# The memory layer of a decode step: the sample's products with the states as tiled matmuls (unsplit fp32 on four column tiles, fp32r on four row tiles)

## The chip, the core and the metric

The kernel runs on one core of one Trainium2 chip. The metric is device time in microseconds (us) of one execution, lower is better. A profile of one execution is shown beside it: its span runs from the first to the last instruction. PE is the matrix engine (PEld its weight loads, which overlap its products), DVE the vector engine, ACT the scalar engine, POOL the general-purpose engine, SP the engine that issues the DMAs here.

## What is computed

One inference step of a two-layer decoder trunk (layer 0: a gated MLP that mixes tokens in chunks; layer 1: an mLSTM matrix memory; a gated MLP with a causal convolution behind each) on a prompt of 256 tokens and on a sample of 8 sequences with 8 new tokens each. All weights are shared. The change lies in layer 1, the memory layer. Per head (8 heads, key width 128, value width 256) the reference does, cut to what matters:

```python
b = jnp.cumsum(fc, axis=-1)
D = where(mask, b[..., :, None] - b[..., None, :] + ic[..., None, :], -inf)
inter = b + m[..., None]
m_t = jnp.maximum(inter, jnp.max(D, axis=-1))
w_intra, w_inter = jnp.exp(D - m_t[..., None]), jnp.exp(inter - m_t)
sc = jnp.einsum('bhtd,bhsd->bhts', qc, kc) * w_intra
num = w_inter[..., None] * einsum('bhtd,bhde->bhte', qc, C) + einsum('bhts,bhse->bhte', sc, vc)
den = w_inter * jnp.einsum('bhtd,bhd->bht', qc, n) + jnp.sum(sc, axis=-1)
h = num / jnp.maximum(jnp.abs(den), jnp.exp(-m_t))[..., None]
g = jnp.exp(bL[..., None] - b + ic - m_new[..., None])
kg = kc * g[..., None]
C_new = decay[..., None, None] * C + jnp.einsum('bhsd,bhse->bhde', kg, vc)
n_new = decay[..., None] * n + jnp.sum(kg, axis=2)
```

The prompt starts from an empty memory. The sample's 8 sequences each bring an old state C (128 x 256 per head) that their 8 queries must meet, and each leaves a new one.

## The kernel before

All activations are kept transposed, 320 tokens wide (256 of the prompt, then 64 of the sample). A weight matrix is used in blocks of 128 output columns: `block` (L151) multiplies 8 slices of 128 x 128 with the activations. fp32 values are split into a high and a low half of type fp32r, and three products (high x high, high x low, low x high) make one fp32 product; that is `chunk` (L143), 24 matmuls of 320 columns for a block. The weights' split is `prefetch` (L104): SP loads a raw block, ACT casts the high half (L125), DVE subtracts for the low half (L126), into three buffers.

The order of the matmuls is the order in which the program issues them (`mm`, `tr` and the helpers pin them). Other instructions are placed by a planner from its own costs; `behind_split` (L130) puts a group behind the last weight split. PSUM has eight banks: three for blocks (`psm`), five for all else (`psa`).

Layer 1 (`layer_b`) first makes the gate rows (`gates`, L508) together with the six blocks of head 0, and then goes through the heads. For head h six blocks are made: two for q and k with a convolution (`qk_epi`), two for v, two for the output gate. Among these blocks stands the memory work of heads h and h - 1:

- `scores` (L628): the decay weights and q k products; it also puts the sample's queries, high half and low half apart, into `Qz`, where each sequence has 128 columns, zero except for its own 8 + 8 rows.
- `state_in`, `state_split` (L704, L711): four loads of two states each, each split by ACT (L715) and DVE (L717) into a high and a low half.
- `inter` (L720): for each sequence two products, `Qz` slice against the high and the low half of its state, 258 columns, into one PSUM bank `num`. 16 matmuls for a head.
- `numer` (L733): 11 products of the scores with the values. `stats` (L747) normalises; `finish` (L813) transposes the result (six transposes) for the out-projection.
- `k_nat`, `v_nat` (L679, L665): keys and values turned to rows. The sample's keys, high halves in partitions 0 to 63 and remainders in 64 to 127, are put into `kgz`: for each sequence a copy with all other rows zero (POOL, L695).
- `state_sample` (L791): for each sequence two products of 256 columns, `kgz` slice against the high and the low half of the values, into a bank `pcs`; DVE adds the decayed old state (L803) and SP stores it. 16 matmuls for a head, four at a time.
- `state_prompt` (L776): the prompt's new state, and the sample's new normaliser with one product of 8 columns (L783).

Head 0 has no work of an earlier head beside it: behind the blocks of `gates` come its three gate transposes `pt` (L585), then at once scores, key and value transposes. Behind the last head the order is: a part of the out-projection, `inter`, `numer`, a block, `stats`, a block, `finish`, `state_sample`.

Of the kernel before, what the change touches and what calls it, by code (L numbers as in the profile page):

```python
# [37 lines left out]
class Net:  # L38
# [10 lines left out]
    def tr(self, out, in_, ident):  # L49
        self.pin(self.nc.tensor.transpose(out, in_, ident))  # L50

# [132 lines left out]

    def tokens(self, a, t):

        return a[:, (0, P, T - P)[t]:(P, TP, T)[t]]

    def norm_cols(self, parts=None, twice=False):
# [4 lines left out]
        pv = pc[:, 0:6].rearrange("p (t e) -> p t e", e=2)  # L194
        for t in range(3):
            for i, a in enumerate(parts):
                self.mm(pv[:, t, :], self.tokens(a, t), self.ones[:, :2], i == 0, i == len(parts) - 1)
# [3 lines left out]
        if twice:  # L201
            nc.scalar.copy(ms[:64, 2:3], ms[64:, 2:3])
        nc.gpsimd.tensor_tensor(rc, ms, self.mhalf.to_broadcast([P, 3]), op=ALU.pow)
        self.rc = rc

    def norm_row(self):
# [4 lines left out]
        for t, (c0, cs) in enumerate(((0, slice(0, P)), (P, slice(0, P)), (TP, slice(64, P)))):  # L211
            nc.vector.tensor_scalar(dg[:, c0:c0 + cs.stop - cs.start], self.ident[:, cs], self.rc[:, t:t + 1], None, op0=MULT)
# [265 lines left out]
    def layer_b(self):  # L478
# [5 lines left out]
        with ExitStack() as ctx:  # L484
# [10 lines left out]
            mk = lp.tile([P, NB], F32, name="mk")  # L495
# [10 lines left out]


            def gates(rp):  # L508
# [4 lines left out]
                RS = rp.tile([P, 384], F32, name="RS")  # L513
# [5 lines left out]
                nc.sync.dma_start(mk, I["blk"])  # L519
                nc.gpsimd.memset(RS, 0.0)  # L520
# [50 lines left out]
                nc.vector.tensor_copy(mkr, mk)  # L571
# [6 lines left out]
                nc.vector.tensor_copy(RS[:, T:384], RS[:, TP:T])  # L578
# [3 lines left out]
                o_epi(0, 1, self.block(KD, self.x_rhs))  # L582
                pt = self.psa.tile([P, 512], F32, tag="pa", name="pt")
                for t in range(3):
                    self.tr(pt[:, t * P:(t + 1) * P], RS[:, t * P:(t + 1) * P], self.ident)  # L585
                nc.vector.tensor_copy(colsT, pt[:, :384].rearrange("p (t e) -> p t e", e=P)[:, :, :96])
                nc.vector.tensor_scalar(colsT[:, :, 32:40], colsT[:, :, 32:40], 0.5 * KSC, None, op0=MULT)

# [3 lines left out]
            def qk_epi(h, j, ps):  # L592
# [16 lines left out]
                qs = lp.tile([P, 384], F32, tag="qs", name="qs", bufs=2)  # L609
# [7 lines left out]
                if j:  # L617
                    nc.scalar.copy(qs[:, T:384], qs[:, TP:T])
# [3 lines left out]
            def v_epi(h, j, ps):  # L622
                vT = lp.tile([P, 384], F32, tag="vT", name="vTb", bufs=2)
                nc.scalar.copy(vT[:, :T], ps[:, :T])
                nc.scalar.copy(vT[:, T:384], ps[:, TP:T])
                S[h].setdefault("vT", []).append(vT)

            def scores(h):  # L628
# [8 lines left out]
                mm(sc[:, 384:448], k[:, TP:384], q[:, TP:T], True, True)  # L637
                w = hp.tile([P, 448], F32, tag="w", name="w", bufs=1)
                for (n, o, c0, c1, t) in ((P, 0, 0, TP, 0), (P, TP, P, TP, 1), (64, 384, TP, T, 2)):
                    nc.scalar.activation(w[:n, o:o + c1 - c0], pb[:n, c0:c1], AF.Exp, scale=-1.0, bias=colsT[:n, t, h:h + 1])  # L640
# [3 lines left out]
                w3 = seg(w[:64, 384:448])  # L644
                nc.gpsimd.affine_select(w3, w3, pattern=[[-NS, NB], [0, NS]], compare_op=ALU.is_ge, fill=0.0, base=0,
                                        channel_multiplier=1)
                nc.gpsimd.affine_select(w3, w3, pattern=[[NS, NB], [1, NS]], compare_op=ALU.is_ge, fill=0.0, base=0,
                                        channel_multiplier=-1)
                dec = hp.tile([P, NB], F32, tag="dec", name="dec", bufs=2)
                nc.vector.tensor_copy(dec, pb[:, 384:392])  # L650
# [8 lines left out]
                nc.vector.scalar_tensor_tensor(Pf[:, :384], sc[:, :384], 0.25 * KSC, w[:, :384], op0=MULT, op1=MULT)  # L659
                nc.vector.scalar_tensor_tensor(Pf[:64, 384:], sc[:64, 384:448], 0.25 * KSC, w[:64, 384:], op0=MULT, op1=MULT)  # L660
                self.split(Ph[:, :384], Pl, Pf[:, :384])
                self.split(Ps[:64, :64], Ps[:64, 64:], Pf[:64, 384:])
                s["P"] = (Ph, Pl, dec)

            def v_nat(h):  # L665
# [6 lines left out]
                for t in range(3):  # L672
                    dst = dsts[t]
                    sc = self.rc[:, t:t + 1]
                    n = P if t < 2 else 64
                    nc.scalar.activation(vh[:, t, :DV], dst[:, :DV], AF.Copy, scale=sc)
                    nc.vector.scalar_tensor_tensor(vl[:n, t, :DV], dst[:n, :DV], sc[:n], vh[:n, t, :DV].bitcast(F32), op0=MULT, op1=SUB)

            def k_nat(h):  # L679
# [3 lines left out]
                for t in range(3):  # L683
                    self.tr(pk[:, t * P:(t + 1) * P], ks[:, t * P:(t + 1) * P], self.ident)
                kgh = hp.tile([P, 2, P], F32R, tag="kgh", name="kgh", bufs=1)
                kgl = hp.tile([P, 2, P], F32R, tag="kgl", name="kgl", bufs=1)
                kgt = hp.tile([P, P], F32R, tag="kgt", name="kgt", bufs=1)
                kgs = hp.tile([P, P], F32R, tag="kgs", name="kgs", bufs=1)
# [143 lines left out]
            with tc.tile_pool(name="rows", bufs=1) as rp:  # L832
                gates(rp)
# [252 lines left out]
```

## Time and profile before

| what | value |
|---|---|
| device time, 3 runs | 980.11, 980.13, 981.29 us (median 980.13) |
| profiled execution, span | 979.3 us |
| lying around the span, against the median | 0.8 us |
| PE busy | 965.4 us (99%) |
| weight loads busy | 959.8 us (98%) |
| DVE, ACT, POOL busy | 701.6, 510.9, 101.8 us (72, 52, 10%) |
| granted PE clock, mean | 0.997 |
| layer 1 in the span | about 432 to 722 us |

The profile gives no other time of the profiled execution than its span. In a timeline a row is the start of an instruction, its length, engine, line, operation, output and inputs, shape, and a count where equal ones follow each other; in square brackets stands how long the engine stood idle before it and what ended that. A matmul's length is longer than its share of the engine, since matmuls are pipelined: what one costs is the distance from its start to the next start. A plain fp32 matmul shows as two instructions with two weight loads, one behind the other.

### The profile page before, as it was taken

What the parts mean: (1) busy time and instruction counts of PE and PEld (TensorE: products, weight loads), DVE (VectorE), ACT (ScalarE), POOL (GpSimd) and SP (SyncE); (2) the same over time, 40 slices, a digit from 0 to 9 for tenths busy, and PEclk for the clock granted to TensorE, in tenths of its full rate; (3) what the DMA queues carried; (4) which work ended last, traced back from release to release, by engine and by line L of the source; (5) the groups of instructions that cost most, each with busy time, mean ns of one, the idle gap of its engine ahead of it and who ended that gap; (6) DMA issues with size and microseconds to landing.
All of it is one profiled execution on the core that took longest, in us unless ns stands there. A gap on an engine that the chain in (4) does not pass through costs nothing.

```text
span 979.3 us, 17600 instructions
## 1 busy us (share of the span) xinstructions
PE 965.4 (99%) x6695; PEld 959.8 (98%) x6695; DVE 701.6 (72%) x1353; ACT 510.9 (52%) x919; POOL 101.8 (10%) x270
## 2 busy tenths in 40 slices
PE   8999999999999999999999999999999999999996
PEld 8999999999999999999999999999999999999996
DVE  6747985567777764458999888788787777775442
ACT  6437444445544543448766766565655455444332
POOL 0200000010000000014332121111101000000000
PEclk9999999999999999999999999999999999999998
DMA  8635444444444455555565655544364444445541
GB/s 276 195 127 158 136 136 152 151 137 152 147 147 153 147 155 149 158 172 169 178 192 177 207 182 167 180 158 152 113 213 155 150 152 151 151 146 148 142 133 54
DMA packets 55802, 154.71 MB, mean 158 GB/s; under 512 B 6614, under 2 KB 17494, under 8 KB 55718
## 3 DMA queue, kind: packets, MB, share of 16 engines
q1 hardware_dynamic: 55718, 153.59, 49.5%
q8 instruction: 53, 0.87, 0.4%
q14 instruction: 31, 0.25, 0.1%
HBM read 141.63 MB, written 11.94 MB: 157 GB/s over the span
## 4 chain that ended last, share of the span: by engine, by line
PE 85%; issue 9%; DVE 2%; DMA 1%; POOL 1%; ACT 1%; SPq 0%; DVEq 0%; POOLq 0%; ACTq 0%
PE pm L47 76%; PE num L47 2%; PE pcs L47 2%; PE pmix L47 1%; DVE wl L126 1%; DMA xT<-in_xT 1%; PE pvt L50 1%; PE phn L50 1%; PE psc L47 1%; PE pCp L47 1%; PE pv L50 0%; DMA C<-in_C 0%; POOL Cl L717 0%; PE pg L47 0%; PE pc L47 0%
## 5 line engine op out<-in xcount | busy, mean ns | idle before, releaser
L125 ACT CAST wh<-raw 128x1024 fp32r<-128x1024 f32 (+3 forms) x254 | 257.5, 1014 | 351.8 <-PE pm L47 198.2
L47 PE MATMUL pm<-xh,wh 128*128 128x320 f32 x1344 | 419.6, 312 | 2.0 <-ACT wh L125 1.8
L47 PE MATMUL pm<-xh,wl 128*128 128x320 f32 x1344 | 415.7, 309 | 0.2 <-DVE wl L126 0.2
L47 PE MATMUL pm<-xl,wh 128*128 128x320 f32 x1344 | 415.3, 309 | 0.0
L126 DVE TENSOR_TENSOR wl<-raw,wh 128x1024 fp32r<-128x1024 f32 (+3 forms) x254 | 303.1, 1194 | 115.9 <-ACT wh L125 113.3
L47 PEld LDWEIGHTS pm<-xh,wh 128*128 128x128 f32 x1344 | 252.6, 188 | 3.1 <-ACT wh L125 2.7
L47 PEld LDWEIGHTS pm<-xh,wl 128*128 128x128 f32 x1344 | 252.3, 188 | 0.7 <-DVE wl L126 0.6
L47 PEld LDWEIGHTS pm<-xl,wh 128*128 128x128 f32 x1344 | 252.6, 188 | 0.2
L47 PE MATMUL pm<-yh_f,wh 128*128 128x320 f32 x352 | 109.0, 310 | 0.0
L47 PE MATMUL pm<-yh_f,wl 128*128 128x320 f32 x352 | 108.5, 308 | 0.0
L47 PE MATMUL pm<-yl_f,wh 128*128 128x320 f32 x352 | 108.5, 308 | 0.0
L47 PEld LDWEIGHTS pm<-yl_f,wh 128*128 128x128 f32 x352 | 66.1, 188 | 0.0
L47 PEld LDWEIGHTS pm<-yh_f,wh 128*128 128x128 f32 x352 | 66.1, 188 | 0.0
L47 PEld LDWEIGHTS pm<-yh_f,wl 128*128 128x128 f32 x352 | 66.1, 188 | 0.0
L400 DVE SCALAR_TENSOR_TENSOR fcv<-fpad,vecs,fcv 128x336 f32<-128x336 f32 x88 | 49.6, 565 | 2.2 <-ACT fcv L398 0.7
L223 DVE TENSOR_TENSOR xT<-pm,xT 128x320 f32<-128x320 f32 x40 | 19.6, 490 | 42.6 <-PE pm L47 42.6
L47 PE MATMUL pm<-yhb,wl 128*128 128x320 f32 x128 | 39.6, 309 | 0.5 <-DVE wl L126 0.5
L47 PE MATMUL pm<-yhb,wh 128*128 128x320 f32 x128 | 39.7, 310 | 0.0
L47 PE MATMUL pm<-yh_a,wh 128*128 128x320 f32 x128 | 39.6, 309 | 0.0
L47 PE MATMUL pm<-ylb,wh 128*128 128x320 f32 x128 | 39.5, 309 | 0.0
L47 PE MATMUL pm<-yh_a,wl 128*128 128x320 f32 x128 | 39.5, 308 | 0.0
L47 PE MATMUL pm<-yl_a,wh 128*128 128x320 f32 x128 | 39.5, 308 | 0.0
(251 smaller groups left out, 1265.6 us busy)
## 6 DMA issues: line engine op xcount, KB each, us to landing
raw<-in_f_up SPq DMA_DIRECT2D x88, 512.0 KB, 3.3
raw<-in_b_win SPq DMA_DIRECT2D x48, 512.0 KB, 3.6
raw<-in_a_win SPq DMA_DIRECT2D x30, 512.0 KB, 3.8
raw<-in_f_dn SPq DMA_DIRECT2D x32, 448.0 KB, 3.4
C<-in_C SPq DMA_DIRECT2D x32, 258.0 KB, 4.1
raw<-in_a_wo SPq DMA_DIRECT2D x16, 512.0 KB, 3.9
raw<-in_f_dn SPq DMA_DIRECT2D x16, 512.0 KB, 3.5
out_Cs<-C SPq DMA_DIRECT2D x32, 256.0 KB, 2.9
```

Source lines behind the costliest of these rows:

```text
L47: self.pin(self.nc.tensor.matmul(out, lhsT, rhs, start=start, stop=stop))
L50: self.pin(self.nc.tensor.transpose(out, in_, ident))
L125: self.last_split = nc.scalar.copy(wh[:, :kn, :], raw[:, :kn, :])
L126: self.last_low = nc.vector.tensor_tensor(wl[:, :kn, :], raw[:, :kn, :], wh[:, :kn, :].bitcast(F32), op=SUB)
L223: self.nc.vector.tensor_tensor(x, ps[:, :T], x, op=ADD)
L400: nc.vector.scalar_tensor_tensor(cv, pd[:, i:i + NC], self.vec(w + i * KF), cv, op0=MULT, op1=ADD)
```

## The change

The sample's 64 tokens are laid out anew wherever they stand in partitions: four groups of 32 partitions, in each 16 tokens (two sequences) twice (`spread`, `twice`). In the lower copy the high halves are to stand, in the upper one the remainders. The mask array `blk` gets five more columns for that, and a new small array `mxb` masks the sample's score weights.

- `inter` takes the states as fp32, unsplit: for each of four groups g and each of its two sequences i one product of 32 query columns against 258 state columns, into partitions 32 g to 32 g + 31 of the bank. That is 8 plain fp32 matmuls for a head, on four column tiles. `state_split` goes away, and with it the halves of the states; `Qz` is fp32 and has 320 columns.
- `state_sample` takes keys and values from 32 partitions: for each sequence of a group and each half of the values one product for each of the four groups, 256 columns, into four PSUM banks at once. 16 fp32r matmuls for a head, on four row tiles. `kgz` goes away; `kz` is made by four DVE instructions.
- The old `state_sample` is cut in two: the matmuls, and `state_out` (DVE and the store).
- `state_prompt` makes the normaliser with two products instead of one.
- The order within a head changes: `inter` and `state_sample` of head h stand together at its end (`hand_over`), `numer` and `state_prompt` behind the first block of the next head (`close`, one block earlier than before), `k_nat` at once behind `scores`, `finish` ahead of an output-gate block instead of behind it. `state_in` stands behind the second block.
- The first block of head 1 is made inside `gates`, ahead of the transposes `pt`.

```diff
+    def tr_some(self, out, in_, ident):
+        self.pin(self.nc.tensor.matmul(out, in_, ident, start=True, stop=True, is_transpose=True))
...
+    @staticmethod
+    def spread(x):
+        return x.rearrange("p (g d s) -> p g d s", g=4, d=2)
+    @staticmethod
+    def twice(x):
+        return x.rearrange("p (g s) -> p g s", g=4).unsqueeze(2).to_broadcast([P, 4, 2, 16])
...
                 o_epi(0, 1, self.block(KD, self.x_rhs))
+                ps = self.block(KD, self.x_rhs)
                 pt = self.psa.tile([P, 512], F32, tag="pa", name="pt")
...
             def scores(h):
-                qw = hp.tile([P, 64], F32, tag="qw", name="qw", bufs=1)
-                nc.vector.scalar_tensor_tensor(qw, q[:, TP:T], 0.5, pb[:, T:384], op0=MULT, op1=MULT)
-                Qd = Qz.rearrange("p (b e) -> p b e", e=136)
-                nc.scalar.copy(Qd[:, :, 0:8], seg(qw))
-                nc.vector.tensor_tensor(Qd[:, :, 64:72], seg(qw), Qd[:, :, 0:8].bitcast(F32), op=SUB)
+                Qd = Qz.rearrange("p (g i r) -> p g i r", g=4, i=2)[:, :, :, :NS]
+                nc.vector.scalar_tensor_tensor(Qd, q[:, TP:T].rearrange("p (g i t) -> p g i t", g=4, i=2), 0.5,
+                                               pb[:, T:384].rearrange("p (g i t) -> p g i t", g=4, i=2), op0=MULT, op1=MULT)
...
             def k_nat(h):
-                nc.gpsimd.tensor_tensor(kgz, kgs.bitcast(F32).unsqueeze(1).to_broadcast([P, NB, P]),
-                                        mk.unsqueeze(2).to_broadcast([P, NB, P]), op=MULT)
+                for i in range(2):
+                    nc.vector.tensor_scalar(kr[:, i, :], src, gm[:, 2 + i, h:h + 1], None, op0=MULT)
+                    nc.vector.scalar_tensor_tensor(kz[:, i, :], src, gm[:, i, h:h + 1], kr[:, i, :].bitcast(F32), op0=MULT, op1=SUB)
...
-            def state_split(h, i):
-                C0 = S[h]["C"][i]
-                Ch = hp.tile([P, 2, CW], F32R, tag="Ch", name="Ch", bufs=3)
-                Cl = hp.tile([P, 2, CW], F32R, tag="Cl", name="Cl", bufs=3)
-                nc.scalar.copy(Ch, C0)
-                (nc.vector if h or i < 2 else nc.gpsimd).tensor_tensor(Cl, C0, Ch.bitcast(F32), op=SUB)
...
+            def inter(h):
+                s = S[h]
+                s["num2"] = self.psa.tile([P, 512], F32, tag="pa", name="num")
+                for i in range(2):
+                    for g in range(4):
+                        mm(s["num2"][32 * g:32 * g + 32, :CW], Qz[:, 80 * g + 32 * i:80 * g + 32 * i + 32], s["C"][g][:, i, :],
+                           i == 0, False)
+            def state_sample(h):
+                s = S[h]
+                kz = s["kg"][2]
+                s["pcs"] = [self.psa.tile([P, 512], F32, tag="pa", name="pcs") for _ in range(4)]
+                for i in range(2):
+                    for v in (vh, vl):
+                        for g in range(4):
+                            r = slice(32 * g, 32 * g + 32)
+                            mm(s["pcs"][g][:, i * DV:(i + 1) * DV], kz[r, i, :], v[r, 2, :DV], v is vh, v is vl)
+            def state_out(h, g):
+                s = S[h]
+                dec, C0, pcs = s["P"][2], s["C"][g], s["pcs"][g]
                 for u in range(2):
+                    b = 2 * g + u
+                    nc.vector.scalar_tensor_tensor(C0[:, u, :DV], C0[:, u, :DV], dec[:, b:b + 1], pcs[:, u * DV:(u + 1) * DV],
+                                                   op0=MULT, op1=ADD)
+                nc.sync.dma_start(O["Cs"][h, :, 2 * g:2 * g + 2, :], C0[:, :, :DV])
...
-                mm(pc[:, 264:272], kgs, mkr, True, True)
+                for i in range(2):
+                    mm(pc[:, 264:272], kz[:, i, :], mkr, i == 0, i == 1)
...
+            def hand_over(h):
+                inter(h)
+                state_sample(h)
+                for g in (0, 1):
+                    state_out(h, g)
+            def close(h):
+                for g in (2, 3):
+                    state_out(h, g)
+                numer(h)
+                state_prompt(h)
+            state_in(0)
+            scores(0)
+            k_nat(0)
+            v_nat(0)
+            for h in range(1, NH):
+                last = h == NH - 1
+                ps = second if h == 1 else blk()
+                if h > 1:
+                    close(h - 1)
+                qk_epi(h, 0, ps)
+                early(h, 0)
+                ps = blk()
+                if h == 1:
+                    hand_over(0)
+                qk_epi(h, 1, ps)
+                early(h, 1)
+                state_in(h)
+                ps = blk()
+                if h == 1:
+                    close(0)
+                else:
                     with self.behind_split():
                         stats(h - 1)
+                v_epi(h, 0, ps)
+                early(h, 2)
+                ps = blk()
+                if h == 1:
+                    with self.behind_split():
+                        stats(0)
+                v_epi(h, 1, ps)
                 scores(h)
+                k_nat(h)
+                if h > 1:
+                    finish(h - 1)
                 early(h, 3)
+                if last:
+                    begin(0)
+                else:
+                    o_epi(h, 0, blk())
+                if h == 1:
+                    finish(0)
                 early(h, 4)
+                v_nat(h)
+                if not last:
                     o_epi(h, 1, blk())
+                    hand_over(h)
                 early(h, 5)
...
             begin(1)
-            inter(h, 1)
-            for i in (2, 3):
-                inter(h, i)
+            inter(h)
             numer(h)
...
             finish(h)
-            for i in range(4):
-                state_sample(h, i)
+            state_sample(h)
+            for g in range(4):
+                state_out(h, g)
             begin(2)
```

More of the change, by code (lines that the diff above doesn't have):

```diff
@@ L701, in k_nat @@
                     nc.vector.scalar_tensor_tensor(kgl[:, t, :], src, g, kgh[:, t, :].bitcast(F32), op0=MULT, op1=SUB)
-                s["kg"] = (kgh, kgl, kgs, kgz)
+                s["kg"] = (kgh, kgl, kz)
             def state_in(h):
@@ L772, in stats @@
                 for t in range(3):
-                    n = P if t < 2 else 64
-                    nc.scalar.activation(hn[:n, t, :], src[t][:n, :DV], AF.Identity, scale=sl[:n, t:t + 1], bias=nb[:n, t:t + 1])
+                    nc.scalar.activation(hn[:, t, :], num[t][:, :DV], AF.Identity, scale=sl[:, t:t + 1], bias=nb[:, t:t + 1])
             def state_prompt(h):
                 s = S[h]
-                kgh, kgl, kgs, kgz = s["kg"]
+                kgh, kgl, kz = s["kg"]
                 dec = s["P"][2]
@@ L890, in layer_b @@
+                v_epi(h, 1, ps)
                 scores(h)
+                k_nat(h)
+                if h > 1:
+                    finish(h - 1)
                 early(h, 3)
-                last = h == NH - 1
-                if h and not last:
-                    o_epi(h, 0, blk())
-                if h:
-                    finish(h - 1)
-                    for i in (2, 3) if last else (2,):
-                        state_sample(h - 1, i)
                 if last:
                     begin(0)
+                else:
+                    o_epi(h, 0, blk())
@@ L901, in layer_b @@
+                if h == 1:
+                    finish(0)
                 early(h, 4)
-                state_in(h)
-                for i in (0, 1):
-                    state_split(h, i)
-                if h and not last:
+                v_nat(h)
+                if not last:
                     o_epi(h, 1, blk())
-                if h and not last:
-                    state_sample(h - 1, 3)
-                if not h:
-                    for i in (2, 3):
-                        state_split(h, i)
```

169 lines of the change are left out of this document (62 added, 107 removed).

## The prediction

> **What bounds the kernel now.** I read first the page's busy line and its slices, then the chain of waits, then a table of stretches over layer 1.
>
> ```profile
> PE 965.4 (99%) x6695; PEld 959.8 (98%) x6695; DVE 701.6 (72%) x1353; ACT 510.9 (52%) x919; POOL 101.8 (10%) x270
> DVE  6747985567777764458999888788787777775442
> PEclk9999999999999999999999999999999999999998
> PE 85%; issue 9%; DVE 2%; DMA 1%; POOL 1%; ACT 1%; SPq 0%; DVEq 0%; POOLq 0%; ACTq 0%
> 432.50:475.50 43.00, 41.32 (x284) 39.66 (x283) 37.17 (x87) 31.43 (x61) 18.23 (x36) 1.00 0.53 171
> 475.50:691.70 216.20, 216.20 (x1570) 216.15 (x1570) 185.58 (x468) 138.27 (x314) 41.29 (x75) 1.00 0.55 175
> 691.70:722.00 30.30, 28.84 (x206) 28.27 (x205) 24.83 (x61) 17.39 (x38) 2.75 (x2) 1.00 0.54 171
> ACT wh L125 <- PE pm L47: 198.2, 98, 3.4
> ```
>
> The stretch rows give, behind the length, the busy time of PE, PEld, DVE, ACT and POOL. PE runs at full clock, and from 475.5 to 691.7 us (heads 1 to 7 but for their ends) it has no idle moment: 216.20 of 216.20 us. The weight split waits for PE's buffers (198.2 us), not PE for it. So in that stretch a nanosecond is won or lost only by what PE itself must do. It idles in two places of layer 1: 1.7 us around head 0 and 1.5 us behind head 7.
>
> What a matmul costs is the distance between starts, not its length:
>
> ```profile
> 695.97 0.28 PE L47 MATMUL num<-Ch,Qz 128*128 128x258 f32 x1
> 697.42 0.28 PE L47 MATMUL num<-vh,Ps 128*128 128x258 f32 x1
> 707.67 0.28 PE L47 MATMUL pcs<-vl,kgz 128*128 128x256 f32 x1
> 709.32 0.28 PE L47 MATMUL pcs<-vl,kgz 128*128 128x256 f32 x1
> 52.14 1.88 PE L47 MATMUL pr<-ws_a,ones 128*128 128x512 f32 x4
> L47 PE MATMUL pr<-ws_a,ones x4: 590/592/592, 52.1 to 53.4; 128*128 128x512 f32 x4
> 32.36 0.70 PE L47 MATMUL pb<-dg,ones 128*128 128x320 f32 x2
> L47 PE MATMUL pb<-dg,ones x8: 430/432/432, 32.4 to 742.0; 128*128 128x320 f32 x8
> 549.42 0.82 PE L50 MATMUL pv<-ident,vTb 128*128 128x128 f32 x6
> L50 PE MATMUL pv<-ident,vTb 128*128 128x128 f32 x48 | 6.6, 274 | 0.0
> ```
>
> Twelve `inter` products lie between 695.97 and 697.42: 0.121 us each. Fourteen steps of `state_sample` lie between 707.67 and 709.32: 0.118 us each. A plain fp32 matmul is two passes (the `pr` row has x4 for two calls, `pb` x2 for one). A pass of 512 columns steps by (1.88 - 0.59) / 3 = 0.43 us, one of 320 by 0.70 - 0.43 = 0.27 us: 0.84 ns for a column, so 0.217 us for 258. The two passes of one call follow each other in the queue. Where the columns are few, the load of 128 weight columns sets the step: (0.82 - 0.27) / 5 = 0.109 us in the value transposes.
>
> **The change part by part.** The sum is made against the profiled execution: span 979.3 us; the median of the runs, 980.13, is 0.8 us more, and I add these 0.8.
>
> *Removed on PE.* 16 products of `inter`, 16 x 0.121 = 1.93 us, and 16 of `state_sample`, 16 x 0.118 = 1.89 us, for each of 8 heads: 30.6 us.
>
> *The new `inter`: 8 fp32 calls, 16 passes of 0.217 us.* No row of before shows a product on part of the array. One after another they take 16 x 0.217 = 3.47 us for a head; four tiles wholly side by side 4 x 0.217 = 0.87. In the loop the two passes of a call come together and need the same tile, so the second must wait for the first; only then can the next group's first pass start, if PE keeps the order of its starts, as all rows of before do. Then a call's second pass runs beside the next call's first: 9 steps, 1.95 us. I take 1.95, since it needs no more than that tiles overlap and that the order is kept; x8 = 15.6 us. Ends 6.9 and 27.7.
>
> *The new `state_sample`: 16 fp32r products, interleaved over the four tiles.* Side by side it is four rounds, 4 x 0.118 = 0.47 us; bound by weight loads of 128 columns, one at a time, 16 x 0.109 = 1.74; as now, 1.89. I take 0.47, because here no neighbour needs the same tile, bank or rows; x8 = 3.8 us. Ends 3.8 and 15.1. The Trainium skill, page "TensorE: Matmul & The Clock Gate", section "LDWEIGHTS (loading the stationary operand)", speaks against it: a load's time goes by its columns, and a load of 32 rows takes as long as one of 128. By that alone the term would be 16 loads in a row and the sum that of the second rival. Its page "TensorEngine Tiling (Array Packing)", section "Key Properties", says that different tiles load and multiply in parallel; by that the sum stands as it is. No run here shows either.
>
> *Changes of the array's form.* From whole array to column tiles, to row tiles and back: three for a head, four in the last, 25 in all. Nothing of the kind is in the trace. If the next product must wait until the last is through, it loses the part of a length that is otherwise overlapped, 0.28 - 0.12 = 0.16 us; at worst a load that could not be made ahead comes on top:
>
> ```profile
> L47 PEld LDWEIGHTS pr<-ws_a,ones x4: 188/188/189, 52.0 to 53.0; 128*128 128x128 f32 x4
> ```
>
> so 0 to 0.35 us each. I take 0.16, the nearest row's: 4.0 us. Ends 0 and 8.7. The Trainium skill, page "TensorEngine Tiling (Array Packing)", section "Key Properties", says that a change of mode drains the engine. By that 0.16 is the right kind of price and the sum stays; without it the sum would be 4.0 us less.
>
> *One more normaliser product* for each head, held by its weight load: 8 x 0.11 = 0.9 us.
>
> PE's own sum: 15.6 + 3.8 + 4.0 + 0.9 - 30.6 = -6.3 us.
>
> *ACT, DVE, POOL.* Rows of what goes, and of DVE in a plain head:
>
> ```profile
> L715 ACT CAST Ch<-C x32: 607/620/632, 461.6 to 693.4; 128x516 fp32r<-128x516 f32 x32
> L717 DVE TENSOR_TENSOR Cl<-C,Ch x30: 665/686/748, 462.7 to 695.7; 128x516 fp32r<-128x516 f32 x30
> 490.80:520.50 29.70, 29.70 (x219) 29.69 (x219) 27.95 (x73) 20.88 (x48) 8.49 (x12) 1.00 0.61 192
> 466.18 1.90 POOL L695 TENSOR_TENSOR kgz<-kgs,mk 128x1024 fp32r<-128x1024 f32 x1 [0.55 <-DVE kgs L694]
> 470.61 0.56 DVE L606 SCALAR_TENSOR_TENSOR bcv<-bpad,vecs,bcv 128x344 f32<-128x344 f32 x1
> 470.35 0.34 DVE L701 SCALAR_TENSOR_TENSOR kgl<-pk,cols,kgh 128x128 fp32r<-128x128 f32 x1
> ```
>
> A head loses 4 x 0.62 us on ACT, 4 x 0.69 on DVE and 1.9 on POOL; DVE gains four key instructions of about 0.34 (the `kgl` row, the same shape) and a few small ones. Worth in time: nothing, since PE waits for none of them; the cover of the new instructions is PE's blocks, and DVE's 27.95 of 29.70 us falls. If a plain head shrinks to 28.7 us, DVE has about 26 in it.
>
> *Head 0.*
>
> ```profile
> 456.54 0.41 PE L50 MATMUL pt<-ident,RS 128*128 128x128 f32 x2 [0.49 <-ACT RS L576]
> 457.51 0.33 PE L50 MATMUL pt<-ident,RS 128*128 128x128 f32 x1 [0.57 <-DVE RS L578]
> 469.40 0.39 PE L47 MATMUL num<-Cl,Qz 128*128 128x258 f32 x1 [0.62 <-POOL Cl L717]
> 457.87 1.75 SPq L708 DMA_DIRECT2D C<-in_C  x4
> DMA to landing us min/median/max: 2.1/3.7/6.8
> 692.79 0.36 PE L47 MATMUL num<-Ch,Qz 128*128 128x258 f32 x1 [0.80 <-ACT kgs L693]
> ```
>
> The block moved ahead of `pt` (3.5 us) covers the two waits, 1.06 us; the wait for `Cl` (0.62) goes with `Cl`. Late next: the state loads, which started at 457.87, when `pt` had freed the rows' memory, start with the later `pt` at about 459.9 and land by 465.4 (last issue 1.75 us on, plus 3.7); `hand_over` is due at about 465.3. (The landing row is that of all transfers of C.) And `state_sample` needs the keys, the values and all five PSUM banks: a good dozen DVE instructions of 0.3 to 0.6 us (the two DVE rows above) between weight splits, some 5 to 9 us, where from `pt` to there 7.4 us pass (459.8 to 465.3, and `inter`). Behind that wait stand all blocks of head 1. I allow 1.0 us, between 0 and 2.3. Head 7: the wait of 0.80 goes, since the states are loaded a head earlier (four more issues of 0.44 us on SP ahead of raw loads that are not awaited); at the end four banks are wanted at once, while two hold transposes: 0.5 us. Net: -1.06 - 0.62 + 1.0 - 0.80 + 0.5 = -1.0.
>
> Sum: 979.3 + 0.8 - 6.3 - 1.0 = 972.8 us.
>
> **The rivals.** *First, slower: fp32 products on column tiles do not overlap.* Then `inter` costs 3.47 instead of 1.95 us, + 12.2 in all: 985.0. It decides from 2.86 us a head on (1.95 + 7.3 / 8). For it: nothing in the trace runs two products side by side, and a pass costs 0.217 against 0.121. Against it: the tiles share neither columns nor partitions of the result.
>
> *Second: weight loads bind the row tiles*, 1.74 instead of 0.47: + 10.2, 983.0. For it: the 0.109 of the `pv` row, which no shorter product undercuts. It turns the sign from 1.38 us a head on. With the first: 995.2.
>
> *Third: all four column tiles run side by side*, 0.87: - 8.6, 964.2. It needs the starts of later calls to pass a waiting second pass.
>
> *Fourth: `finish` comes too early.* It now stands one output block nearer to `stats`:
>
> ```profile
> 596.99 0.29 PE L47 MATMUL num<-vh,Pl 128*128 128x258 f32 x1
> 607.42 0.59 ACT L774 ACTIVATE hn<-ns,nb,sl 64x256 f32<-64x256 f32 x1
> 613.97 0.82 PE L50 MATMUL phn<-ident,hn 128*128 128x128 f32 x6
> ```
>
> The normalised rows are ready 608.01 - 597.28 = 10.7 us behind `numer`. In the new order about 12.7 us lie between (`state_prompt` 0.9, three blocks of 3.5, scores and key transposes 1.3): 2 us to spare. If the lag grew by 3 us, six heads would wait 1 us each, and by 3.2 or more the gain is gone: about 980.
>
> **How the numbers follow.** Chances: forecast 0.36 (its own range, from the ends of the changes of form and of head 0: 968 to 978), second 0.22, first 0.14, first and second together 0.11, third 0.10, fourth 0.07. The range 962 to 988 takes in the third, the forecast, the fourth, the second and most of the first; the two slow ones together stay out. A measurement of this kernel tells about 0.2% (2 us) from no change. Faster: 0.36 + 0.10 + a part (0.04) of the second, where changes of form are cheap, + 0.02 of the fourth = 0.52. Within 0.2%: 0.09, from the second, first and fourth. Slower: 0.39.
>
> **What would show it.** The starts of the eight `num` calls on `C`: 9 steps of 0.22 us (forecast), 16 (first), 4 (third). The starts of the sixteen `pcs` products: bunches of four within some ns and four rounds of 0.12, or a steady 0.11. The gap ahead of the first `num`, first `pcs` and the block behind: 0.16. No idle ahead of `pt`; idle ahead of `phn` would be the fourth. The prediction is wrong if partial products take other times than whole ones.

## The result and the profile after

| | before | after |
|---|---|---|
| device time, median | 980.36 us (979.05 to 981.84) | 977.74 us (975.44 to 979.85) |
| ratio | | 0.9972, 95% interval 0.9961 to 0.9983 |
| executions | 10 | 10 |
| profiled execution, span | 979.3 us | 975.8 us (its time 977.89) |

The change makes the kernel 2.6 us faster, where 7.3 us were forecast. The sign and the range held; the gain was about a third of the forecast. (The executions of before with a known span lie 1.9 us above it, so the profiled one of before took about 981.2 us, not the median that I put it at; the changed kernel lies 2.1 us above its span.)

The page's busy line of the changed kernel, and stretches of it (behind the length: PE, PEld, DVE, ACT and POOL busy, then the granted clock):

```profile
PE 957.5 (98%) x6703; PEld 941.0 (96%) x6703; DVE 686.7 (70%) x1344; ACT 484.6 (50%) x846; POOL 71.9 (7%) x238
430.00:436.00 6.00, 4.76 (x29) 4.21 (x28) 4.48 (x9) 2.82 (x5) 2.38 (x9) 0.94 0.77 236
435.30:438.60 3.30, 3.30 (x13) 3.30 (x14) 0.89 (x5) 1.04 (x1) 0.85 (x1) 0.50 0.85 276
478.00:507.00 29.00, 25.30 (x196) 23.41 (x195) 23.63 (x66) 13.77 (x36) 3.25 (x6) 1.00 0.63 201
507.00:690.00 183.00, 181.86 (x1377) 175.67 (x1376) 150.60 (x388) 103.47 (x220) 16.74 (x48) 1.00 0.53 176
```

Before, PE had no idle moment from head 1 to head 7. Now it idles 3.7 us in 29 us of head 1, 1.1 us in heads 2 to 7, and 1.2 us in the gates, behind which 3.3 us run at half clock. All engines have less to do, and PE waits more.

The tiles themselves did better than forecast. The end of a block, `inter`, `state_sample` and the start of the next block in a plain head of the changed kernel (start, length, and the count in one row), with the weight loads below:

```profile
553.20 0.31 PE L47 MATMUL pm<-xh,wl 128*128 128x320 f32 x1
553.43 1.08 PE L47 MATMUL num<-C,Qz 128*32 128x258 f32 x16
554.45 0.39 PE L47 MATMUL pcs<-vh,kz 32*128 32x256 f32 x4
554.67 0.29 PE L47 MATMUL pcs<-vl,kz 32*128 32x256 f32 x4
554.78 0.29 PE L47 MATMUL pcs<-vh,kz 32*128 32x256 f32 x4
554.90 0.28 PE L47 MATMUL pcs<-vl,kz 32*128 32x256 f32 x4
555.12 0.42 PE L47 MATMUL pm<-xh,wh 128*128 128x320 f32 x1
555.37 0.31 PE L47 MATMUL pm<-xl,wh 128*128 128x320 f32 x1
...
554.67 0.19 PEld L47 LDWEIGHTS pcs<-vh,kz 32*128 32x128 f32 x4
```

Sixteen passes of `inter` take 1.02 us to the next start (554.45 - 553.43): four rounds of 0.20 to 0.22 and one change of form. The sixteen products of `state_sample` come in rounds of four, 0.12 us apart behind a first of 0.22, and four loads of 128 columns, each 0.19 long, lie in one row: they run at once. From 553.35, where the next block product would have started (553.20 + 0.147), to 555.12 pass 1.77 us, in place of the 3.82 removed.

The new pauses, from the timelines of the changed kernel (in brackets the idle time and what ended it), and DVE's queue ahead of the first:

```profile
433.42 1.22 DVE L130 TENSOR_TENSOR wl<-raw,wh 128x1024 fp32r<-128x1024 f32 x1
434.56 0.47 DVE L567 TENSOR_TENSOR gr<-pg,gr 64x320 f32<-64x320 f32 x1
434.96 0.21 DVE L210 COPY acc<-acc 128x128 f32<-128x128 f32 x1
435.22 0.58 PE L47 MATMUL pc<-ones,acc 128*128 128x2 f32 x2 [1.24 <-DVE acc L210]
469.08 2.76 PE L47 MATMUL num<-C,Qz 128*32 128x258 f32 x15 [0.86 <-DMA C<-in_C]
484.39 0.44 PE L50 MATMUL pk<-ident,qs 128*128 128x128 f32 x2 [1.24 <-ACT w L678]
489.29 0.79 PE L50 MATMUL phn<-ident,hn 128*128 128x128 f32 x2 [0.84 <-ACT hn L801]
495.97 0.39 PE L47 MATMUL pcs<-vh,kz 32*128 32x256 f32 x3
497.72 0.38 PE L47 MATMUL pcs<-vh,kz 32*128 32x256 f32 x1 [1.36 <-DVE vl L706]
543.72 0.39 PE L47 MATMUL psc<-qh,kh 128*128 128x256 f32 x1 [0.20 <-ACT kh L251]
607.80 0.39 PE L47 MATMUL psc<-qh,kh 128*128 128x256 f32 x1 [0.48 <-ACT kh L251]
693.02 0.41 PE L47 MATMUL pm<-ylb,wh 128*128 128x320 f32 x1 [0.26 <-DVE ylb L840]
```

Counted as distance between starts beyond the usual step, so with the slower step behind each pause, they cost: gates 1.4 us and the half clock behind it 1.5; head 0 1.0 ahead of `inter` and 1.9 inside it, where its tiles wait for one load after the other; head 1 1.4, 1.7 and 1.6; `kh` in heads 2 to 6 2.9 together (from `pMb` to the last score product 0.55, 0.55, 0.55, 0.84 and 0.44 more than the 0.81 of before); around the out-projection's start 1.4. Sum 14.8. The waits of before that went (`pt` 1.4, `Cl` 0.8, `kgs` 1.0) give 3.2 back: 11.6 us more waiting than before.

Two of the pauses in head 1 are waits for a PSUM bank. `pk` does not read `w`, and the fourth `vh` product of `pcs`, which stands still while three others have started, does not read `vl`. By the kernel's text three `num`, `pMb` and `psc` hold the five banks of `psa` when `pk` wants one, and ACT makes `w` from `pMb`; at the fourth `pcs` they are held by `num`, three `pcs` and a `pv`, from which DVE makes `vl`. So such a pause lasts until a late ACT or DVE has read a bank, and the four banks that `state_sample` takes at once are part of its cause. This is worked out from the rows and the kernel; no run has more banks.

### The profile page after: what moved, and what is told of

It reads as the page before. It is cut to its first block, busy times and chain, and to the rows that moved or that the text cites. A ratio compares the mean times of both kernels' runs of the same rounds, so it can differ in the third digit from the quotient of the medians.

```text
span 975.8 us, 17507 instructions
## 1 busy us (share of the span) xinstructions
PE 957.5 (98%) x6703; PEld 941.0 (96%) x6703; DVE 686.7 (70%) x1344; ACT 484.6 (50%) x846; POOL 71.9 (7%) x238
```

## The experiments

The theory behind the first runs: the tiles save what four full rounds promise, and the gain was lost to waits made by the new order of work. Rivals: the tiles owe their speed to the order of the calls; the waits come from DMA; DVE and ACT limit PE whatever the order. Ratios are to the kernel before, run beside each.

**The order of the calls in `inter`.**

```diff
-                for i in range(2):
-                    for g in range(4):
+                for g in range(4):
+                    for i in range(2):
```

> One edit of the changed kernel: the two loops of inter change places, so that both sequences of a column tile follow one another before the next tile's. The same 8 fp32 products a head, in another order. Theory (a start in program order holds back all later ones): a tile's second product must wait for the two passes of its first, and the tiles behind it wait too; of 16 passes about 13 steps of 0.22 us are left instead of 4, 2.8 us a head instead of 0.9, about +15 us in all, 993 us. Rival (each column tile has a queue of its own, which later products reach past a waiting one): the four tiles still run side by side, 0.9 us a head, 977.7 us as before the edit.

977.35 us, ratio 0.9974 (0.9964 to 0.9984): no difference to the changed kernel. The same place in a plain head (the row with x4 counts the passes that start in the first 0.1 us, the one with x16 all):

```profile
552.09 0.31 PE L47 MATMUL pm<-xh,wl 128*128 128x320 f32 x1
552.33 0.45 PE L47 MATMUL num<-C,Qz 128*32 128x258 f32 x4
552.33 1.10 PE L47 MATMUL num<-C,Qz 128*32 128x258 f32 x16
553.36 0.39 PE L47 MATMUL pcs<-vh,kz 32*128 32x256 f32 x4
```

Four passes start at once and the sixteen take 1.03 us, though each tile's four passes now stand one behind the other in the program. That the chip got the new order shows in head 0, where the states come one by one: four passes 0.22 us apart stand between two waits for a load, where the changed kernel has two. So a product that waits for its own tile does not hold those of other tiles. My reason for 9 steps falls.

**The column tiles' worth.** The 8 products of a head on the whole array, with zero columns (`Qz` is larger for that and is filled by two instructions, not shown).

```diff
-                for i in range(2):
-                    for g in range(4):
-                        mm(s["num2"][32 * g:32 * g + 32, :CW], Qz[:, 80 * g + 32 * i:80 * g + 32 * i + 32], s["C"][g][:, i, :],
-                           i == 0, False)
+                for b in range(NB):
+                    mm(s["num2"][:, :CW], Qz[:, b * P:(b + 1) * P], s["C"][b // 2][:, b % 2, :], b == 0, False)
```

> One part of the change undone: the states stay unsplit fp32, but each of the 8 products of a head takes the whole array (128 query columns, zero except for its own), as before the change, instead of one of four column tiles. Theory (the four column tiles run fully side by side and are worth three quarters of the time): 16 passes of 0.22 us one after the other, 3.5 us a head instead of 0.9 to 1.0, less one change of array form of 0.1; 2.4 us a head, 8 heads, +19 us: 997 us. Rival (the unsplit products by themselves bring most of it, a pass of 258 columns costing about the 0.12 us of an fp32r product): 1.9 us a head, +8 us: 986 us.

991.85 us, ratio 1.0114 (1.0100 to 1.0129).

```profile
555.79 3.65 PE L47 MATMUL num<-C,Qz 128*128 128x258 f32 x16
559.38 0.39 PE L47 MATMUL pcs<-vh,kz 32*128 32x256 f32 x4
468.70 4.11 PE L47 MATMUL num<-C,Qz 128*128 128x258 f32 x16 [0.58 <-DMA C<-in_C]
```

3.59 us a head instead of 1.02, as in theory, 16 x 0.22. The total rose by 14 us, not 19: in head 0 `inter` took 2.9 us anyway, waiting for its states, and in head 1 the pauses ahead of `phn` and inside `pcs` are gone, probably because DVE got more time (not tested). Some 2 us of the difference stay open. Without the column tiles the rest of the change, row tiles included, makes the kernel slower than before.

**The wait in the gates.**

```diff
-            nc.vector.tensor_copy(self.spread(acc2), self.twice(self.acc[:, TP:]))
+            nc.scalar.copy(self.spread(acc2), self.twice(self.acc[:, TP:]))
```

> One edit of the changed kernel: the second half of the gate scan's copy (acc2 in L210), for which the pc matmul in the gates waits, is made by ACT instead of DVE, where it stands behind the low half of a weight block (1.22 us) and another instruction. Theory (a queue on DVE and a clock that falls behind the pause): the wait of 1.24 us at 433.7 us goes and with it the 3.4 us at half clock behind it; gates end about 2.9 us earlier, the whole about 974.8 us against 977.7 of the changed kernel. Rival (the half clock does not hang on this pause): the half-clock record stays or falls elsewhere, and at most 1.2 us are gained. Second rival (ACT is itself behind a cast of 1.4 us there): no gain.

975.50 us, ratio 0.9957 (0.9945 to 0.9969), some 1.5 to 2.2 us below the changed kernel; the two intervals overlap, so the size is not firm. (ACT's casts there take 1.05 us; the 1.4 of the second rival stands in no row.)

```profile
433.38 1.10 PE L47 MATMUL pc<-ones,acc 128*128 128x2 f32 x6
```

The six products stand in one row, without the pause. The half clock went from the gates, but stands in this profile behind the pause in `pcs` of head 1 instead. So it is shown that the pause came from DVE's queue; that the half clock hangs on this pause alone is not shown.

**The state loads.** `state_in(h)` put behind `k_nat` and `finish` in the program.

```diff
                 early(h, 1)
-                state_in(h)
...
                     finish(h - 1)
+                state_in(h)
```

> One edit of the changed kernel: the four loads of old states of a head (state_in) are issued behind the fifth block's place (behind k_nat and finish) instead of behind the second block. Theory (the state loads delay a raw weight block, whose cast on ACT stands ahead of kh): the cast of wh ahead of kh no longer waits 1.75 us for its DMA, the pauses of psc for kh (0.20, 0.20, 0.20, 0.48, 0.07 us in heads 2 to 6, about 2.9 us with the slower starts behind them) go, about 975 us. Rival (ACT and DVE have too much to do between the second block and the scores, whatever the loads do): the kh pauses stay within 0.1 us, 977.7 us; if the states then come late for inter, more: up to +0.5 us a head, 982 us.

978.31 us, ratio 0.9977 (0.9964 to 0.9989). SP's rows in head 4, of the changed kernel and of this one:

```profile
561.66 0.35 SPq L734 DMA_DIRECT2D C<-in_C  x1
563.09 0.45 SPq L114 DMA_DIRECT2D raw<-in_b_wo  x1
```

```profile
562.44 0.35 SPq L734 DMA_DIRECT2D C<-in_C  x1
563.88 0.45 SPq L114 DMA_DIRECT2D raw<-in_b_wo  x1
```

The planner put the loads, and all else, where they had been. The run decides nothing on the loads of plain heads; it is a second measurement of the changed kernel.

**Head 1.** `stats(0)` right behind `close(0)`, `k_nat(1)` behind `finish(0)`.

```diff
                 if h == 1:
                     close(0)
-                else:
-                    with self.behind_split():
-                        stats(h - 1)
+                with self.behind_split():
+                    stats(h - 1)
...
-                if h == 1:
-                    with self.behind_split():
-                        stats(0)
...
-                k_nat(h)
                 if h > 1:
+                    k_nat(h)
                     finish(h - 1)
...
                 if h == 1:
                     finish(0)
+                    k_nat(1)
```

> One edit of the changed kernel, in head 1 alone: the normaliser work of head 0 (stats) comes right behind close(0), as in the later heads, and head 1's key transposes come behind finish(0). Theory (five PSUM banks are full in head 1, because the three banks num of head 0 are held until stats): the pause of 1.24 us ahead of pk and the one of 0.84 us ahead of phn go, and head 1 ends 2 to 4 us earlier, about 974 to 976 us. Rival (DVE, busy 31 of 36 us there, is what holds head 1): the pauses move on to vl and into head 2, gain below 1 us.

976.67 us, ratio 0.9957 (0.9945 to 0.9969), some 1 to 1.5 us below the changed kernel, with overlapping intervals: between the theory and the rival. DVE's work is the same, and the pauses ahead of `pk` and in `pcs` went, which fits waits for a bank; the one ahead of `phn` grew:

```profile
485.81 0.78 PE L50 MATMUL phn<-ident,hn 128*128 128x128 f32 x2 [1.50 <-ACT hn L801]
```

The first edit and this one together (`x9_acc_head1`):

> Two edits together: the gate scan's second copy on ACT, and in head 1 stats right behind close and the key transposes behind finish. Theory (two separate waits): the gains of the single edits (2.2 and 1.1 us) add, 974.4 us against 977.7 of the changed kernel. Rival (a head that starts 2.9 us earlier meets later transfers, so that the pause ahead of inter of head 0 or in head 1 grows): 975.5 us, as with the first edit alone.

973.55 us, ratio 0.9929 (0.9917 to 0.9941). Together they bring at least the sum of the two.

**Is DVE behind head 1?** The eight products of `state_out` are left out for head 0; PE's work stays.

```diff
-                for u in range(2):
+                for u in range(2 if h else 0):
```

> The changed kernel, without the eight DVE instructions of state_out in head 0 alone (L762, 0.42 to 0.48 us each, some 3.5 us of DVE between 472.7 and 478 us): head 0's new sample states are stored without the product, so this part of the computation is left out. PE's work is the same. Theory (DVE's backlog in head 1, where it is busy 31 of 36 us, holds hn, w and vl): the pauses of head 1 (1.24 us ahead of pk, 0.84 ahead of phn, 1.36 inside pcs, 4.8 us with the slow steps behind) shrink to under 1 us together, 973 to 974 us. Rival (what holds PE there is the order: the banks held until stats, and hn and w behind weight casts on ACT): at least the pauses ahead of pk and phn stay, under 1.5 us gained, 976.5 us or more.

973.03 us, ratio 0.9918 (0.9904 to 0.9931): 4.7 us below the changed kernel, from 3.5 us less work on DVE. Head 1 in both, the changed kernel first:

```profile
468.00:504.00 36.00, 31.35 (x245) 27.10 (x244) 30.36 (x82) 16.98 (x39) 5.01 (x9) 1.00 0.66 222
```

```profile
468.00:504.00 36.00, 35.30 (x280) 31.83 (x279) 31.98 (x90) 19.66 (x48) 5.55 (x11) 1.00 0.77 242
483.19 0.44 PE L50 MATMUL pk<-ident,qs 128*128 128x128 f32 x2
487.09 0.38 PE L50 MATMUL phn<-ident,hn 128*128 128x128 f32 x2
493.03 0.39 PE L47 MATMUL pcs<-vh,kz 32*128 32x256 f32 x4
```

All three pauses are gone. So head 1's waits, 4.7 us, hang on head 0's state products: eight of them (0.42 to 0.48 us each) now come close together behind head 0, amid the convolution. Whether it is DVE's time alone is not shown: without these products the four `pcs` banks come free at once, too.

**One part of the order undone:** `close` behind the second block again.

```diff
-                if h > 1:
-                    close(h - 1)
                 qk_epi(h, 0, ps)
...
                 if h == 1:
                     hand_over(0)
+                else:
+                    close(h - 1)
```

> One part of the order undone in heads 2 to 7: the products numer and the prompt's state (close) of the head before stand behind the second block again instead of behind the first; inter and state_sample stay at the head's end. ACT then casts kh ahead of the three hn of 1.48 us. Theory (hn and a weight cast stand ahead of kh in ACT's queue): the pauses of psc for kh (0.20, 0.20, 0.20, 0.48 us, about 2.4 us with the slower step behind each) go, 975.3 us against 977.7 of the changed kernel. Rival (the time between second block and scores is too short whatever the order): the pauses move to hn or to the key transposes and nothing is gained, 977.7 us; above that, to 980 us, if the three banks num, held one block longer, stop a block.

981.12 us, ratio 1.0002 (0.9991 to 1.0013): the rival, and worse. The pauses for `kh` went, as the theory had it, but the key transposes, which stand right behind the scores, now wait until `hn` has been made from the three `num` banks, 0.26 us in each of heads 2 to 6, and the last head has longer pauses:

```profile
517.03 0.44 PE L50 MATMUL pk<-ident,qs 128*128 128x128 f32 x2 [0.26 <-ACT hn L801]
692.27 0.41 PE L50 MATMUL pv<-ident,vTb 128*128 128x128 f32 x2 [0.87 <-DVE Pf L687]
```

**The tiles in an order near the old one.**

```diff
-                    close(h - 1)
+                    hand_over(h - 1)
                 qk_epi(h, 0, ps)
...
                 if h == 1:
                     hand_over(0)
+                else:
+                    close(h - 1)
                 qk_epi(h, 1, ps)
...
                     o_epi(h, 0, blk())
-                if h == 1:
-                    finish(0)
+                    finish(h - 1)
+                    k_nat(h)
                 early(h, 4)
-                v_nat(h)
+                state_in(h)
                 if not last:
                     o_epi(h, 1, blk())
-                    hand_over(h)
+                v_nat(h)
```

In head 1 `stats(0)` stands right behind `close(0)` too, as in the run on head 1 (not shown).

> The tiles of the change with an order of work near to that before: inter and state_sample stand behind the first block of the next head, numer and the prompt's state behind the second (in head 1 behind the second and third), finish and k_nat behind an output-gate block, state_in behind that. Theory (the new waits in the heads come from the new order, not from the tiles): the pauses of head 1 (1.24, 0.84, 1.36 us, 4.8 us with the slower steps behind) and those for kh (2.9 us) go, the one in the gates stays; 977.7 - 7.7 = 970 us. Rival (DVE and ACT are near their limit and hold PE wherever the work stands): pauses of the same sum at other places, 975 us or more.

970.80 us, ratio 0.9893 (0.9878 to 0.9908): 10 us below before, 7 below the changed kernel.

```profile
505.00:686.00 181.00, 180.98 (x1379) 175.89 (x1378) 150.25 (x391) 100.53 (x223) 18.40 (x49) 1.00 0.56 182
527.51 1.08 PE L47 MATMUL num<-C,Qz 128*32 128x258 f32 x16
555.37 1.08 PE L47 MATMUL num<-C,Qz 128*32 128x258 f32 x16
488.56 0.78 PE L50 MATMUL phn<-ident,hn 128*128 128x128 f32 x2 [1.50 <-ACT hn L801]
```

Heads 2 to 7 have no idle moment again, and a plain head takes 27.86 us (555.37 - 527.51) in place of 29.70: 1.84 us less. That is what the change is worth on PE where nothing waits; taken for all 8 heads, 14.7 us. Left are the gates, head 0's loads and `phn` in head 1. Which of the moves is needed is not taken apart; that of `close` alone is not enough.

**On from there.** With the copy on ACT (`x7_late_acc`):

> The tiles in the older order (the run before with 970.8 us), and besides it the gate scan's second copy on ACT. Theory: the pause of 1.25 us in the gates goes, and the 3.4 us at half clock that mostly follow it; as with that edit alone 2.2 us less, 968.6 us. Rival (the half clock falls behind the next pause instead, the 1.5 us one ahead of phn in head 1, anyway): 1.2 us less, 969.6 us.

969.58 us, ratio 0.9900 (0.9883 to 0.9917): no difference that the intervals show. The pause in the gates went, but `inter` of head 0, reached earlier, now waits at its start. The group's row over all heads, with its idle time at the end, names ACT; but the third load of the states lands at 469.39 us and the third tile's products start at 469.43, so it is the loads:

```profile
L47 PE MATMUL num<-C,Qz 128*32 128x258 f32 x128 | 10.5, 387 | 1.2 <-ACT wh L129 1.0
```

With `finish(0)` behind the second output-gate block besides (`x12_late_acc_fin`):

> As the run with the older order and the copy on ACT, and besides it finish(0) in head 1 stands behind the second output-gate block instead of the first. Theory (hn of head 0 is late since ACT casts a weight block ahead of it, and a block of 3.5 us covers that): the pause of 1.50 us ahead of phn goes, with the two slow steps behind it (0.69 us) and the 3.4 us at half clock that follow (1.4 us lost): 3.0 to 3.5 us less, 965.3 us. Rival (the pause moves to the next consumer, the value transposes): under 1 us less, 968 us.

970.41 us, ratio 0.9898 (0.9882 to 0.9915): no gain, as the rival had it. The pause ahead of `phn` went and came back not at the value transposes but in `state_sample`, where the fourth product waits for the bank that DVE makes `vl` from:

```profile
495.93 0.39 PE L47 MATMUL pcs<-vh,kz 32*128 32x256 f32 x1 [1.36 <-DVE vl L706]
```

With the state loads in a pool of their own, ahead of the gates (`x13_cpool`):

```diff
+            cb = ctx.enter_context(tc.tile_pool(name="cb", bufs=1))
+            state_in(0)
             with tc.tile_pool(name="rows", bufs=1) as rp:
                 second = gates(rp)
...
-            state_in(0)
             scores(0)
```

> As the run before it (older order, copy on ACT, finish(0) later), and besides it the four state loads of head 0 are put ahead of the gates, into a pool of their own, so that they don't stand behind two raw weight loads on SP. Theory (the states of head 0 land too late): the pauses inside inter of head 0 (0.13, 0.32, 0.63 us, 1.7 us with the slow steps) go, inter of head 0 takes 0.9 us instead of 2.8: 1.7 us less, 963.7 us. [...]

967.46 us, ratio 0.9873 (0.9859 to 0.9888). The 963.7 us of the theory are not reached. `inter` of head 0 runs without a wait, in 1.0 us. Behind it stand two new pauses for a bank, which DVE is late to read, and the pause in head 1 stays:

```profile
464.85 1.08 PE L47 MATMUL num<-C,Qz 128*32 128x258 f32 x16
466.75 0.39 PE L47 MATMUL pcs<-vh,kz 32*128 32x256 f32 x1 [0.50 <-DVE kgl L727]
473.26 0.36 PE L47 MATMUL pCp<-vh,kgh 128*128 128x258 f32 x1 [0.73 <-DVE C L755]
493.83 0.38 PE L47 MATMUL pcs<-vh,kz 32*128 32x256 f32 x1 [1.36 <-DVE vl L706]
```

This version beats both kernels: 12.5 us below before, 10 below the changed kernel. How much of the 2.9 us to the last run is the loads' is open: the two intervals just overlap, and the last run's profile has a stretch at half clock behind its pause in `pcs` (496.9 to 500.3 us), this one none. What is left are mainly these three waits for a bank.

## Why the prediction was right and wrong

- *Removed on PE, 30.6 us:* right; with the new work a head falls by 1.84 us where nothing waits.
- *`inter`, 1.95 us a head:* too high. The third rival's mechanism held, four full rounds, 0.88 us; x8 = 7.0 us instead of 15.6. The failed step is "if PE keeps the order of its starts"; the run with the loops changed shows that it does not across column tiles.
- *`state_sample`, 0.47:* right, four rounds of 0.12. The second rival fell: a load of 32 rows and 128 columns is as long as one of 128 rows (0.19 us), but four run at once. Of the two pages weighed there, the Trainium skill's "TensorEngine Tiling (Array Packing)", section "Key Properties", agrees with the trace: tiles load in parallel.
- *Changes of form, 0.16 each:* right in size: 0.09 ahead of the column tiles, 0.10 to the row tiles, some 0.1 in the first step there, and 0.1 each ahead of and behind the next block's first product; 0.5 a head, 4.0 in all.
- *PE's own sum, -6.3:* it was -30.6 + 7.0 + 3.8 + 4.0 + 0.9 = -14.9, beside the 14.7 taken from a plain head in the order near the old one.
- *Relief of ACT and DVE worth nothing, its cover PE's blocks:* this is the step that failed most. I looked at busy time of a plain head (28 of 29.7 us) and not at what the moved pieces meet. With less of PE's work between second block and scores, and eight state products in one place, DVE and ACT became late at points, while their totals fell. PSUM banks I counted in heads 0 and 7 alone; in head 1 two of the three pauses, 1.4 and 1.6 us, are waits for one.
- *Waits, net -1.0:* about +11.6, as listed. `pt`, `Cl` and `kgs` went as forecast. Head 0 cost 2.9 (allowed: 1.0, at most 2.3). I took its loads to start at 459.9 and to land 3.7 us behind their issue, by 465.4; they started at 463.43, most of it from the gates' pause and half clock, which put `inter` off as well, and came one after the other until about 471, the third 5.9 us behind its issue. The "blocks of head 1 behind it" did wait, in head 1 itself, 4.7 us. The copy `acc2` in the gates, one DVE instruction of the full diff that the shown part leaves out, was not in the sum at all: 1.4 us and, in the profile, 1.5 of half clock.
- *Fourth rival, `finish` too early:* the right place and the wrong victim. In the plain heads `phn` never waited; but `hn`, early on ACT, stood ahead of `kh`. In the order near the old one these waits are gone.

That the forecast was near is luck: two errors of opposite sign, -8.6 on the tiles and +12.6 on the waits, partly met. By the span, 979.3 - 14.9 + 11.6 = 976.0, against 975.8 measured; each term is read to about 0.1 us, so nothing large is left over. The likeliest case had 0.36, while the third rival, with the right mechanism, had 0.10 and, at 964.2, lies 3 us from the version in which the waits are mostly gone.

## What to carry to other kernels

Price the moved work at the point where its consumer stands, not by an engine's busy share: list, for each moved group, what now stands ahead of the next thing that PE needs in DVE's and ACT's queues. Where a faster piece and a new order come in one change, measure the piece in the old order first; here the order alone ate 7 of 10 us. When one pause is removed, look for the next consumer of the same queue, and for the next tile that wants a PSUM bank: four of the edits here moved a pause, and the last, which removed one at its cause, left two smaller ones behind it.

## What was not expected of the hardware

- Four fp32 column tiles run as if each had a queue of its own: sixteen passes in 1.02 us against 3.59 on the whole array, in either order of the calls. The Trainium skill, page "TensorE: Matmul & The Clock Gate", section "The mechanism" of its Part 3, says that matmuls start and end strictly in program order; the run with the loops changed, where the four tiles still start together, does not agree.
- Four weight loads of 128 columns on row tiles run at once (four of 0.19 us in one row).
- The half clock. Where PE paused for 1.15 us or more in layer 1, a stretch of 3.4 us at a granted clock of 0.50 followed in some executions and not in others: behind 11 of 26 such pauses in all the profiles here, and nowhere else in layer 1. With the same 1.25 us pause in the gates, the run with the loops changed had none:

```profile
435.44 0.38 PE L47 MATMUL pc<-ones,acc 128*128 128x2 f32 x2 [1.25 <-DVE acc L210]
435.50:439.00 3.50, 3.50 (x25) 3.50 (x26) 0.89 (x5) 1.05 (x1) 0.85 (x1) 1.00 0.74 277
```

  Where the pause falls matters. In the clock records of every profile here the changes of the clock lie whole multiples of 3.413 us apart. Of the 26 pauses, 19 leave 1.15 us or more of idle time in one window of that grid, and all 11 stretches follow such a window; the other 7, which a boundary divides into smaller parts, had none. The pause shown is one of the 7, with 0.43 and 0.82 us. Why 8 of the 19 had none is open.

  Each such stretch costs about 1.7 us, an estimate from half its length (1.5 in the gates of the changed kernel), and with it the spread goes: the executions of the changed kernel reach from 975.44 us at a mean clock of 0.998 to 979.85 at 0.991, those of before lie at 0.995 to 0.998. So a pause can cost more than its length. The Trainium skill, page "TensorE: Matmul & The Clock Gate", section "Part 1: The HAM clock gate (the "warmup" mystery)", gives a free-running window of 3413 ns: the length and the grid agree. Its rule of no idle gaps beyond about 3.4 us (section "HAM oscillation — how this bites in real kernels") is too weak here: 1.15 us in one window were enough.
